# A hybrid decoder block: cross-attention's transposes one step later, three PSUM banks for attention's output product, and the second feed-forward product's first operands in another order

## Chip, cores and metric

The kernel runs on one core of a Trainium2 chip. The metric is device time in microseconds, the median of the runs of one program. A core has TensorE (matmuls, here PE, with its weight loads PEld), VectorE (DVE), ScalarE (ACT), GpSimd (POOL) and SyncE (SP), whose queue issues nearly all DMAs of this kernel. Each engine takes its instructions in the order of its own queue.

## The reference, cut to what matters

One layer on a sequence of 1024 tokens of width 1024, with 256 memory tokens, all in float32:

```python
u = rms_norm(h, norm_mix);  proj = u @ w_in            # parts for both branches and the gates
out_a = GLU of a diagonal state-space branch
att   = forgetting_attention(q, k, v, f_logit)          # 8 heads of 64
out_b = att @ w_fox_o                                   # "attention's output product"
h = h + (gate_a * out_a + gate_b * out_b) @ w_mix_out   # "mix product"
n = rms_norm(h, norm_mem_q); m = rms_norm(mem, norm_mem_kv)
s = (n @ w_q)(m @ w_k)^T * 128**-0.5                    # 4 heads of 128, 256 memory tokens
h = h + (softmax(s) @ (m @ w_v)) @ w_mem_o              # cross-attention
f_a, f_b = split(rms_norm(h, norm_ffn) @ w_ffn_in)      # first feed-forward product
h = h + (silu(f_a) * f_b) @ w_ffn_out                   # second feed-forward product, 2816 x 1024
out = rms_norm(h, norm_final)
```

## The kernel before

Every float32 matrix product is made of three matmuls: each operand is split into a high half, a cast on ScalarE (L178), and a low half, the subtraction source minus high half, mostly on VectorE (L179). L168, L169 and L170 are the three: high by high, high by low, low by high. PSUM has eight banks of 128 x 512, handed out by name: three "mm", two "sc", two "pv" and one "misc". A bank goes to its next user when its last reader is done.

The program is written in an order that a planner then re-arranges. The planner knows estimated costs, and puts on each engine's queue what it takes to be ready, earlier written work first. After that the order on a queue is fixed. `B.behind(ins)` adds one rule for it: the instructions of the block that run on the engine of `ins` come behind `ins` in that queue; DMAs and the other engines are not bound by it.

**Attention's output product** (`fox_part`, L525 to L539) runs in eight parts of 128 output channels, each in two units of 512 tokens. A unit is 12 matmuls into one bank `po`. VectorE multiplies the bank by the gate (L536), which frees the bank, and adds the other branch (L537); the sum is split into `mx`, the operand of the mix product. The two units of a part take the two "pv" banks in turn. Beside it GpSimd applies the other branch's gates (L1131), and ScalarE and VectorE split the weights of the mix product; the first half of them lies in tiles `whi` and `wlo`, four of each, which the output product's weights use as well.

**Cross-attention** (`cross`) works on two halves of 512 tokens. A half has eight steps, two pairs of heads by four blocks of 128 tokens. A step is `mem_scores` (6 matmuls into an "mm" bank; row maximum on VectorE, L687; two exponentials with sums on ScalarE, L690; reciprocal on VectorE, L692; normalising on GpSimd, L694) and `mem_turn` (four transposes into the "misc" bank, L703, split into `pth` and `ptl`). After the four steps of a pair of heads, `mem_values` multiplies by the values. The first half is woven with the query product of the second half, the second half with the memory output product (`mem_out`, sums at L729) of the first. Then the next normalisation (L193 to L220) and the sums and differences for the first feed-forward product follow.

**The feed-forward products** use a recursive scheme with seven half-size products in place of eight. The first one runs over `NF` = 22 blocks of 128 hidden channels, in `start`, `middle` and `end` (matmuls at L875); `middle` ends with a copy of a bank on ScalarE (L896), which `end` needs before it may go on adding into that bank. The hidden values go to DRAM (`gated`: L925, L932), and sums of the second weights as well (`out_sums`: L946, L947).

The second product takes 77 operands in the order of `seq`: `o_get(m)` loads the hidden values (L998) and the weights (L1004) with two DMAs into a tile `or` and splits it; `o_mm` makes 12 matmuls of it (L1015), three into each of four banks. The first seven operands are asked for before its loop starts, four of them ahead of the last block's `end`:

```python
    for m in range(4):
        o_get(m)
    end(NF - 1)
    for m in range(4, AHEAD):       # AHEAD = 7
        o_get(m)
    gated(NP - 1)
    out_sums(NP - 1, 1)
    gfin = B.bcast_gain(s2, g_fin)
```

and the loop asks for operand `m + AHEAD` when it has done operand `m`.

Of the kernel before, what the change touches and what calls it, by code (L numbers as in the profile page):

```python
# [502 lines left out]
def stage_tail(B, big, s2, sh, x, glu, aT, gate_d, kv_d, w_fox_o, w_mix_out, g_mq, w_mem_q, w_mem_o, g_ffn,  # L503
               w_ffn_in, w_ffn_out, g_fin, out):
    nc, V, A, G, T, S, small, ident = B.nc, B.V, B.A, B.G, B.T, B.S, B.small, B.ident
# [19 lines left out]
    def fox_part(j):  # L525
        if j % 2 == 0:
            fox[j // 2] = B.wblock(w_fox_o, 0, 4, j * P, 2 * P)
        fh, fl = fox[j // 2]
        o = (j % 2) * P
        sg = glu.out.pop(j)  # L530
        for h in range(2):
            cs = slice(512 * h, 512 * h + 512)
            po = B.bank("pv")
            B.gemm_t(po, fh[:, :, o:o + P], fl[:, :, o:o + P], aT, h, 4)
            gb = load(gate_d[D + j * P:D + (j + 1) * P, cs], "gb")
            V.tensor_mul(gb, gb, po)  # L536
            V.tensor_add(sg[:, cs], sg[:, cs], gb)  # L537
            mh, ml = mT.rhs(j, h)
            B.split(mh, ml, sg[:, cs])  # L539
# [8 lines left out]
    for j in range(5, 8):  # L548
        fox_part(j)
# [147 lines left out]
    def mem_turn(hf, b, tt):  # L697
        pe = pes.pop((hf, b, tt))
        if tt == 0:
            pts[b] = [(tmp("pth", F32R), tmp("ptl", F32R)) for _ in range(2)]  # L700
        pt = B.bank("misc")
        for i in range(4):
            T.transpose(pt[:, i * P:(i + 1) * P], pe[:, i * P:(i + 1) * P], ident)  # L703
        for i in range(2):
            hi, lo = [p_.rearrange("p (k c) -> p k c", k=2)[:, :, tt * P:(tt + 1) * P] for p_ in pts[b][i]]
            B.split(hi, lo, pt[:, 2 * i * P:2 * (i + 1) * P].rearrange("p (k c) -> p k c", k=2))

    def mem_values(hf, b):
        if b == 0:
            oT[hf] = [[(bslot if hf else slot)(F32R, n) for _ in range(2)] for n in ("oh", "ol")]  # L710
        oh, ol = oT[hf]
        for i in range(2):
            ps = B.bank("pv")
            for kt in range(2):
                cs = slice(kt * 512 + (2 * b + i) * P, kt * 512 + (2 * b + i + 1) * P)
                ks = slice(512 * kt, 512 * kt + 512)
                B.mm3(ps, vh[:, cs], vl[:, cs], pts[b][i][0][:, ks], pts[b][i][1][:, ks], kt == 0, kt == 1)
            B.split(oh[b][:, i * 512:(i + 1) * 512], ol[b][:, i * 512:(i + 1) * 512], ps)
# [12 lines left out]
    def cross(hf):  # L731
        steps = [(b, tt) for b in range(2) for tt in range(4)]
        fs = []
        for i in range(len(steps) + 1):
            if i < len(steps):
                fs.append(lambda s=steps[i]: mem_scores(hf, *s))
            if i > 0:
                fs.append(lambda s=steps[i - 1]: mem_turn(hf, *s))
                if steps[i - 1][1] == 3:
                    fs.append(lambda b=steps[i - 1][0]: mem_values(hf, b))  # L740
        return fs

    for i, s_ in enumerate((kth, ktl, vh, vl)):
# [143 lines left out]
    def middle(j):  # L887
        b1 = ev[j, "b1"]
        b3 = ev[j, "b3"] = B.bank("pv")
        prod(j, 6, b1, False)  # L890
        a1 = ev[j, "a1"] = sh.half("a1")
        A.copy(a1, b1)
        prod(j, 7, b3, True)
        prod(j, 5, b1, False)
        c1 = ev[j, "c1"] = sh.half("c1")
        A.copy(c1, b1)  # L896
        V.scalar_tensor_tensor(out=c1, in0=c1, scalar=-1.0, in1=b3, op0=ALU.mult, op1=ALU.subtract)

    def end(j):
        b1, b3, a0, a1, c1 = [ev.pop((j, s_)) for s_ in ("b1", "b3", "a0", "a1", "c1")]  # L900
# [72 lines left out]
    for j in range(2, NF):  # L973
        if j > AHEAD_IN:
            start(j)
        end(j - 1)
        w_last(j)
        middle(j)
        if j + 1 < NF:
            w_first(j + 1)  # L980
            w_sums(j + 1)
        f = w_fetch(j + 2) if j + 2 < NF else f
        if j % 2:
            out_fetch(j // 2, f.ins)
        else:
            gated(j // 2 - 1)


    LAST, AHEAD = 4, 7
    ORDER = (1, 2, 6, 7, 5, 4, 3)  # L990
    seq = [(n, p) for n in ORDER for p in range(NP)]
    ops, Hf, fin = {}, {}, {}
# [62 lines left out]
                                   op1=ALU.mult)  # L1055
            S.dma_start(out[t * P:(t + 1) * P, cs], Hf[t][:, cs])

    for m in range(4):
        o_get(m)
    end(NF - 1)  # L1060
    for m in range(4, AHEAD):
        o_get(m)
    gated(NP - 1)
    out_sums(NP - 1, 1)
    gfin = B.bcast_gain(s2, g_fin)
# [1 line left out]
    for m, (n, p) in enumerate(seq):  # L1067
        if n == 3 and p >= NP - LAST:
            break
        for i in range(4):  # L1070
            o_mm(m, i)
        if m + AHEAD < len(seq):
            o_get(m + AHEAD)
        if n < 3 and p in (2, 4, 6, 8):
            t = 4 * (n - 1) + p // 2 - 1
            Hf[t] = slot(name="hf")
            S.dma_start(Hf[t], h_d[t])
        if p == NP - 1:
            for i in range(4):
                o_add(n, i)  # L1080
                if n in (2, 5):
                    square(i if n == 2 else 4 + i, n // 3)
                if n == 2:
                    G.tensor_mul(Hf[i][:, :512], Hf[i][:, :512], gfin[:, :512])
                if n == 4:
                    square(4 + i, 0)
                    finish(4 + i)
# [758 lines left out]
```

## Time and profile before

| | |
|---|---|
| median of 3 runs | 1579.52 us (1578.55 to 1581.72) |
| the profiled execution | 1578.99 us |
| its span, first to last instruction | 1577.3 us |
| granted TensorE clock, mean | 0.990 |
| TensorE busy | 1529.5 us, 97% |
| VectorE, ScalarE, GpSimd busy | 1023.0, 657.7, 264.9 us |

In the rows of the profile, times are in us from the start of the span. A row of the timeline gives start, duration, engine, line, operation, the tile written and those read, the shape, a count, and in brackets how long the engine was idle before it and what released it. A row of the chain of waits gives start, duration and work. A row of the busy times by stage begins with a stretch A:B and its length; then come, for PE, PEld, DVE, ACT and POOL, the busy us with the number of instructions in brackets, and at the end the granted TensorE clock, the share of the DMA engines' time and GB/s. A row of the waits names waiter and releaser, the idle time in all, how often, and the longest.

### The profile page before, as it was taken

What the parts mean: (1) busy time and instruction counts of PE and PEld (TensorE: products, weight loads), DVE (VectorE), ACT (ScalarE), POOL (GpSimd) and SP (SyncE); (2) the same over time, 40 slices, a digit from 0 to 9 for tenths busy, and PEclk for the clock granted to TensorE, in tenths of its full rate; (3) what the DMA queues carried; (4) which work ended last, traced back from release to release, by engine and by line L of the source; (5) the groups of instructions that cost most, each with busy time, mean ns of one, the idle gap of its engine ahead of it and who ended that gap; (6) DMA issues with size and microseconds to landing.
All of it is one profiled execution on the core that took longest, in us unless ns stands there. A gap on an engine that the chain in (4) does not pass through costs nothing.

```text
span 1577.3 us, 20371 instructions
## 1 busy us (share of the span) xinstructions
PE 1529.5 (97%) x7313; PEld 1258.4 (80%) x7313; DVE 1023.0 (65%) x1822; ACT 657.7 (42%) x1177; POOL 264.9 (17%) x343
## 2 busy tenths in 40 slices
PE   7799999999999899999999999999999999999997
PEld 6688888898777578878888788888888888788886
DVE  6756545444788677676455688777777775566555
ACT  6422434323566553232335565333333332354342
POOL 3026653200212124110001200100000000001001
PEclk8999999999999999999999999999999999999999
DMA  8753466332123746368411156554445543896642
GB/s 295 151 106 97 130 116 143 97 119 30 25 45 56 206 121 194 114 206 284 144 28 40 62 206 192 169 164 158 159 155 162 161 148 130 279 391 223 192 155 107
DMA packets 196101, 235.09 MB, mean 149 GB/s; under 512 B 35144, under 2 KB 127208, under 8 KB 195488
## 3 DMA queue, kind: packets, MB, share of 16 engines
q1 hardware_dynamic: 188512, 215.97, 46.6%
q10 hardware_dynamic: 7488, 17.83, 3.0%
q8 instruction: 57, 0.93, 0.2%
q14 instruction: 44, 0.36, 0.1%
HBM read 162.98 MB, written 72.71 MB: 149 GB/s over the span
## 4 chain that ended last, share of the span: by engine, by line
PE 80%; DVE 7%; DMA 5%; ACT 3%; POOL 2%; issue 2%; SPq 0%; POOLq 0%; ACTq 0%; DVEq 0%
PE mm L875 14%; PE mm L168 8%; PE mm L169 8%; PE mm L170 8%; PE pv L875 7%; PE mm L1015 4%; PE sc L875 4%; PE sc L168 3%; PE sc L170 3%; PE sc L169 3%; PE sc L1015 3%; PE pv L1015 3%; PE misc L1015 1%; DMA raw<-in_w_in_dram 1%; DMA raw<-in_w_mem_kv_dram 1%
## 5 line engine op out<-in xcount | busy, mean ns | idle before, releaser
L178 ACT CAST whi<-raw 128x1024 fp32r<-128x1024 f32 (+2 forms) x123 | 114.7, 940 | 176.7 <-PE mm L875 52.8
L179 DVE TENSOR_TENSOR wlo<-raw,whi 128x1024 fp32r<-128x1024 f32 (+2 forms) x120 | 127.7, 1069 | 73.2 <-ACT whi L178 71.3
L168 PE MATMUL mm<-uh,whi 128*128 128x512 f32 x344 | 137.5, 400 | 2.5 <-ACT whi L178 2.4
L179 DVE TENSOR_TENSOR ol<-or,oh 128x1024 fp32r<-128x1024 f32 x73 | 92.1, 1266 | 68.5 <-ACT oh L178 67.5
L170 PE MATMUL mm<-uh,wlo 128*128 128x512 f32 x344 | 135.2, 393 | 0.5 <-DVE wlo L179 0.5
L169 PE MATMUL mm<-ul,whi 128*128 128x512 f32 x344 | 135.4, 394 | 0.0
L178 ACT CAST oh<-or 128x1024 fp32r<-128x1024 f32 x73 | 76.9, 1053 | 104.5 <-PE mm L1015 35.2
L907 POOL TENSOR_TENSOR g<-a,c 128x512 f32<-128x512 f32 x22 | 35.8, 1627 | 386.8 <-ACT a L906 299.0
L1665 POOL TENSOR_TENSOR pl<-pf,ph 128x512 fp32r<-128x512 f32 (+1 forms) x32 | 37.8, 1181 | 242.7 <-DVE ph L1664 173.1
L168 PEld LDWEIGHTS mm<-uh,whi 128*128 128x128 f32 x344 | 65.2, 190 | 14.8 <-ACT whi L178 2.8
L170 PEld LDWEIGHTS mm<-uh,wlo 128*128 128x128 f32 x344 | 64.9, 189 | 14.7 <-DVE wlo L179 1.5
L169 PEld LDWEIGHTS mm<-ul,whi 128*128 128x128 f32 x344 | 65.2, 190 | 11.0
L197 POOL TENSOR_TENSOR r<-ms,mhalf 128x1 f32<-128x1 f32 (+1 forms) x30 | 19.4, 647 | 308.1 <-DVE ms L193 280.8
L1662 ACT ACTIVATE pf<-sc 128x512 f32<-128x512 f32 (+1 forms) x96 | 46.3, 489 | 45.0 <-DVE sc L1658 29.4
L875 PE MATMUL pv<-S3h,we 128*128 128x512 f32 x176 | 57.7, 389 | 0.0
L1131 POOL TENSOR_TENSOR sg<-sg,ga 128x512 f32<-128x512 f32 x16 | 30.5, 1928 | 72.7 <-DVE sg L1124 72.7
L1668 DVE TENSOR_TENSOR pl<-pf,ph 128x512 fp32r<-128x512 f32 (+2 forms) x64 | 35.8, 560 | 10.5 <-ACT ph L1667 9.7
L1015 PE MATMUL mm<-oh 128*128 128x512 f32 x106 | 41.2, 389 | 0.0
L1015 PE MATMUL mm<-ol,oh 128*128 128x512 f32 x106 | 41.2, 389 | 0.0
L1015 PE MATMUL mm<-oh,ol 128*128 128x512 f32 x106 | 41.2, 389 | 0.0
L178 ACT CAST we<-rawb 128x512 fp32r<-128x512 f32 x20 | 12.5, 624 | 68.9 <-PE pv L875 33.8
L168 PE MATMUL sc<-uh,whi 128*128 128x512 f32 x104 | 40.8, 393 | 0.0
(583 smaller groups left out, 4585.0 us busy)
## 6 DMA issues: line engine op xcount, KB each, us to landing
or<-c_d SPq DMA_DIRECT2D x77, 256.0 KB
raw<-in_w_in_dram SPq DMA_DIRECT2D x22, 512.0 KB
wo<-in_w_ffn_out_dram SPq DMA_DIRECT2D x22, 512.0 KB
c_d<-g SPq DMA_DIRECT2D x44, 256.0 KB
t_d<-wo SPq DMA_DIRECT2D x44, 256.0 KB
or<-t_d SPq DMA_DIRECT2D x44, 256.0 KB
rawb<-in_w_ffn_in_dram SPq DMA_DIRECT2D x20, 512.0 KB
raw<-in_w_ffn_in_dram SPq DMA_DIRECT2D x20, 512.0 KB
```

The source lines that it names most:

```text
L168: T.matmul(ps, lh, rh, start=first, stop=False)
L169: T.matmul(ps, lh, rl, start=False, stop=False)
L170: T.matmul(ps, ll, rh, start=False, stop=last)
L178: self.A.copy(hi, src)
L179: (self.G if pool_lo else self.V).tensor_sub(lo, src, f32(hi))
L875: T.matmul(ps, l_[:, k, :], r_, start=first and k == 0 and i == 0, stop=k == 3 and i == 2, skip_group_check=True)
L907: G.tensor_mul(g[:, 512:], a1, c1)
L1015: T.matmul(ps, l_[:, gi], r_[:, 512:], start=n < 3 and p == 0 and k == 0 or n == 7 and p == 0 and k == 0, stop=p == NP - 1 and k == 2, ski ...
L1131: self.B.G.tensor_mul(self.out[j][:, cs], self.out[j][:, cs], ga)
L1662: self.exp = A.activation(pf[:, off:], ps[:, off:], AF.Exp)
L1665: G.tensor_sub(pl[:, off:], pf[:, off:], f32(ph[:, off:]))
L1668: V.tensor_sub(pl[:, off:], pf[:, off:], f32(ph[:, off:]))
```

## The change

1. A unit of attention's output product takes its bank from "pv", "pv" and "misc" in turn, in place of "pv" alone.
2. In the written order of cross-attention, the transposes of a step (and the value product after every fourth) come two steps after its scores, in place of one. Eight steps of scores and eight of transposes remain.
3. Of the second feed-forward product's operands, three (0 to 2) are asked for as before. Operands 3 to 7 are asked for ahead of the last `end`, with their casts behind the last `middle`'s copy in ScalarE's queue; operand 8 right after that `end`, also behind the copy. The loop asks from operand 9 on, so nine operands are asked for before it in place of seven.

```diff
@@ fox_part
-            po = B.bank("pv")
+            po = B.bank(("pv", "pv", "misc")[(2 * j + h) % 3])
@@ cross
-        for i in range(len(steps) + 1):
+        for i in range(len(steps) + 2):
             if i < len(steps):
                 fs.append(lambda s=steps[i]: mem_scores(hf, *s))
-            if i > 0:
-                fs.append(lambda s=steps[i - 1]: mem_turn(hf, *s))
-                if steps[i - 1][1] == 3:
-                    fs.append(lambda b=steps[i - 1][0]: mem_values(hf, b))
+            if i > 1:
+                fs.append(lambda s=steps[i - 2]: mem_turn(hf, *s))
+                if steps[i - 2][1] == 3:
+                    fs.append(lambda b=steps[i - 2][0]: mem_values(hf, b))
@@ middle
-        A.copy(c1, b1)
+        copied = A.copy(c1, b1)
         V.scalar_tensor_tensor(out=c1, in0=c1, scalar=-1.0, in1=b3, op0=ALU.mult, op1=ALU.subtract)
+        return copied
@@ the loop over the blocks
-        middle(j)
+        copied = middle(j)
@@ before the second feed-forward product
-    LAST, AHEAD = 4, 7
+    LAST, AHEAD, EARLY = 4, 7, 9
...
-    for m in range(4):
+    for m in range(3):
         o_get(m)
+    with B.behind(copied):
+        for m in range(3, 8):
+            o_get(m)
     end(NF - 1)
-    for m in range(4, AHEAD):
-        o_get(m)
+    with B.behind(copied):
+        o_get(8)
     gated(NP - 1)
...
-        if m + AHEAD < len(seq):
+        if EARLY <= m + AHEAD < len(seq):
             o_get(m + AHEAD)
```

## The prediction

> **What bounds the kernel now.** I read the page's first part, the waits of TensorE from 550 us on (all three edits lie there), the busy time by stage, and then the rows around each wait. The page:
>
> ```profile
> PE 1529.5 (97%) x7313; PEld 1258.4 (80%) x7313; DVE 1023.0 (65%) x1822; ACT 657.7 (42%) x1177; POOL 264.9 (17%) x343
> ```
>
> TensorE is the bound, so the edits can only pay by removing time in which it stands still. The view of waits, from 550 us to the end (waiter and releaser, us in total, times, longest):
>
> ```profile
> PE mm L875 <- ACT c L896: 1.7, 2, 1.0
> PE pv L168 <- DVE gb L536: 1.7, 2, 1.2
> PE misc L703 <- POOL pe L694: 1.3, 4, 0.5
> PE misc L703 <- DVE ptl L179: 1.1, 1, 1.1
> ...
> PE mm L168 <- ACT pe L690: 0.3, 1, 0.3
> ```
>
> Each edit has its row here: the second is the output product's (L536 reads the "pv" bank), the third to fifth are cross-attention's, half of the first is the hand-over from the first feed-forward product to the second. Two rows of TensorE give the true price of a wait:
>
> ```profile
> 1302.06 2.72 PE pv L875 x12
> 703.27 0.50 PE L168 MATMUL pv<-ath,whi 128*128 128x512 f32 x1 [1.24 <-DVE gb L536]
> ```
>
> Twelve 512-column matmuls take 2.72 us, 0.227 us each, while a row shows a matmul as some 0.39 us long. So a wait costs the idle time shown plus 0.16 us, plus 0.11 us because the first matmul after it takes 0.50 instead of 0.39: 0.27 us on top, and I use that throughout. Now part by part.
>
> **The output product's third bank.** Nothing is added or removed; every third unit of 12 matmuls goes to the "misc" bank, which nobody else uses at that time (the next transposes into it come some 70 us later). So a unit waits for the bank of the unit three before it and no longer for that of two before it. Both waits go at their place:
>
> ```profile
> 693.55 0.50 PE L168 MATMUL pv<-ath,whi 128*128 128x512 f32 x1 [0.44 <-DVE gb L536]
> ```
>
> 0.44 + 1.24 + 2 x 0.27 = 2.2 us. But is that work late next? The rows of the chain, then VectorE and ScalarE, then VectorE's busy time in this stretch:
>
> ```profile
> 690.52 3.52 POOL sg L1131 x2
> 694.43 5.25 DMA raw<-in_w_mix_out_dram
> 715.62 0.28 PE mm L169
> 700.79 1.23 DVE L179 TENSOR_TENSOR wbl<-raw,wbh 128x1024 fp32r<-128x1024 f32 x1 [2.21 <-ACT wbh L178]
> 711.17 0.62 ACT L178 CAST mxh<-sg 128x512 fp32r<-128x512 f32 x1 [1.30 <-DVE sg L537]
> 711.70 1.04 ACT L178 CAST whi<-raw 128x1024 fp32r<-128x1024 f32 x1
> 714.12 1.22 DVE L179 TENSOR_TENSOR wlo<-raw,whi 128x1024 fp32r<-128x1024 f32 x1
> 700.80:715.30 14.50, 13.26 (x59) 10.56 (x57) 14.40 (x20) 6.86 (x9) 0.00 (x0) 1.00 0.97 312
> ```
>
> The bank comes late because VectorE stands 2.21 us in front of a weight split whose DMA landed at 699.68, and that DMA was queued on SP behind a gate load that waited for GpSimd. None of it hangs on the banks. From 700.8 on VectorE is busy 14.40 of 14.50 us, and near the end of this row of work it makes the low half of the last weights of the mix product, 714.12 to 715.34. TensorE reads those at 715.62, 0.28 us later. If TensorE ends the output product 2.2 us earlier and VectorE keeps its order, TensorE arrives at the same weights 2.2 us earlier and waits there. So I put this edit at 0: the wait moves from 703 to about 713. Ends: 2.2 us gained if VectorE's order is re-planned so that the split comes earlier; 1.5 us lost (a second wait like that at 703.27, 1.24 + 0.27) if it is re-planned badly. I take 0 because the last row fixes it: VectorE has 0.1 us to spare.
>
> The Trainium skill, "Perfetto Trace Analysis", section "Matmuls", has the rule for this edit: independent groups should rotate through different PSUM banks, so that one group's evacuation overlaps the next group's matmuls. By it the whole 2.2 us would stay and the sum below would be lower by that much; it is the first rival.
>
> **Cross-attention's transposes.** Score group i (6 matmuls of 256 columns, maximum, exponentials, normalising on GpSimd) is followed by its four transposes one group later in the written order, and two groups later after the change. The number of instructions is the same, no DMA moves, and the planner still picks what is ready. The waits:
>
> ```profile
> 840.98 0.66 PE L703 MATMUL misc<-ident,pe 128*128 128x128 f32 x4 [0.54 <-POOL pe L694]
> 869.83 0.38 PE L168 MATMUL mm<-kv,mqh 128*128 128x256 f32 x1 [0.25 <-ACT pe L690]
> 880.98 0.66 PE L703 MATMUL misc<-ident,pe 128*128 128x128 f32 x4 [0.23 <-POOL pe L694]
> 885.57 0.63 PE L703 MATMUL misc<-ident,pe 128*128 128x128 f32 x4 [1.12 <-DVE ptl L179]
> 889.27 0.66 PE L703 MATMUL misc<-ident,pe 128*128 128x128 f32 x4 [0.34 <-POOL pe L694]
> 899.13 0.66 PE L703 MATMUL misc<-ident,pe 128*128 128x128 f32 x4 [0.20 <-POOL pe L694]
> 839.88 3.04 POOL L694 TENSOR_TENSOR pe<-pe,sm 128x512 f32<-128x512 f32 x3 [34.78 <-DVE sm L692]
> ```
>
> Together 2.68 + 6 x 0.27 = 4.3 us, the most that can come. The first stays: GpSimd's three multiplications in a row show that three score groups were out before the first transposes already, so the written order changes nothing there (0.81 us). The second is a score group waiting for a bank, which the change does not touch (0.52 us). The three small ones of the second half (0.20 to 0.34 us idle) are shorter than a score group in between (6 x 0.113 us, half the price of 512 columns), so they go: 0.77 + 3 x 0.27 = 1.6 us. The large one, 1.39 us, came because VectorE ran a normalisation before the split that frees the one "misc" bank; one group later takes about half of it, 0.7 us. Against that stands the end of each half: the last three transposes, not two, now follow with no scores between them, through one bank.
>
> ```profile
> 902.62 0.60 PE L703 MATMUL misc<-ident,pe 128*128 128x128 f32 x4
> 905.19 0.63 PE L703 MATMUL misc<-ident,pe 128*128 128x128 f32 x4
> 907.13 0.42 DVE L179 TENSOR_TENSOR ptl<-misc,pth 128x256 fp32r<-128x256 f32 x1 [0.44 <-ACT pth L178]
> ```
>
> One turn holds the bank from 905.19 to 907.55, 2.4 us. Its cover is the other matmuls that are ready, 24 of the memory output product in the second half, 5.4 us, and as many of the query product in the first; without that cover an extra turn costs the 2.4 us in each half. I charge 0.5 us for a cover that is not perfect. Sum: 1.6 + 0.7 - 0.5 = 1.8 us gained; ends 4.3 gained and the third rival's loss.
>
> **The hand-over.** ScalarE's rows, with those of TensorE, of the queue and of the chain (the row with a stretch counts the matmuls of L1015 in it, 7):
>
> ```profile
> 1349.09 2.81 DMA or<-in_w_ffn_out_dram
> 1352.00 1.05 ACT L178 CAST oh<-or 128x1024 fp32r<-128x1024 f32 x1 [4.19 <-DMA or<-in_w_ffn_out_dram]
> 1352.95 0.58 ACT L896 COPY c<-mm 128x512 f32<-128x512 f32 x1
> 1353.58 0.50 PE L875 MATMUL mm<-S4h,wdh 128*128 128x512 f32 x1 [0.97 <-ACT c L896]
> 1350.80:1353.50 2.70, 1.75 (x7) 1.15 (x7) 1.00 0.70 205
> 1368.91 0.42 SPq L1004 DMA_DIRECT2D or<-in_w_ffn_out_dram  x1
> 1374.77 1.05 ACT L178 CAST oh<-or 128x1024 fp32r<-128x1024 f32 x1 [14.06 <-DMA or<-in_w_ffn_out_dram]
> 1375.85 1.24 DVE ol L179
> 1377.13 0.50 PE L1015 MATMUL sc<-ol,oh 128*128 128x512 f32 x1
> ```
>
> The copy at L896 must be done before the last two products of the first stage can start. It stood in ScalarE's queue behind a cast that waited for a DMA until 1351.90, so TensorE, which had filled in seven matmuls of the second product, still lost 0.97 + 0.27 = 1.24 us. After the change the casts of operands 3 to 8 stand behind the copy: the wait goes, and the fill covers the copy's 0.58 us. What now queues behind the copy: six casts of 1.05 us (6.3 us) and six subtractions of 1.24 us (7.4 us). TensorE first needs operand 3 after two products and 36 matmuls, 60 x 0.227 = 13.6 us later, one more operand each 2.72 us; covered. The SiLU of the last block may wait for one cast, 1.05 us; what it feeds is read a whole product later.
>
> Operands 7 and 8, four DMAs, move on SP's queue from behind the last stores and the load of the final gain to ahead of them. Before, operand 7's weights were issued at 1368.91 and its split ended at 1377.09, so TensorE lost 0.13 us of idle time plus 0.27: 0.4 us, which goes. Operand 9 then is the first behind those stores; issued as before near 1369 and ready by 1377.1, it is needed at about 1380.7 (the products end at 1353.58 + 24 x 0.227 - 1.24 = 1357.8, then come nine operands of 2.72 us less the seven matmuls done ahead): 3.6 us to spare. Sum 1.64 us; I take 1.5. Ends: 1.65 gained, 1.2 lost (the copy's wait again, behind a cast that the planner put wrongly).
>
> **The sum.** 0 + 1.8 + 1.5 = 3.3 us. The profiled execution took 1578.99 us (span 1577.3 and 1.7 around it), so 1575.7; the median of the runs is 0.5 above that execution, so 1576.2. Does a gain at 900 reach the end? Stages after it:
>
> ```profile
> 828.00:909.40 81.40, 78.73 (x414) 64.03 (x415) 48.88 (x125) 43.74 (x131) 18.51 (x20) 1.00 0.16 60
> 926.00:965.00 39.00, 38.74 (x187) 31.91 (x186) 37.17 (x83) 24.19 (x62) 1.48 (x2) 1.00 0.72 245
> 947.00:1346.00 399.00, 398.28 (x1758) 329.39 (x1757) 287.81 (x416) 148.94 (x250) 31.96 (x20) 1.00 0.51 163
> ```
>
> VectorE is full from 926 to 965 (37.17 of 39 us), but with work that TensorE's results start, so it shifts along; after it TensorE runs without holes for 399 us at half the DMA's capacity.
>
> **Rivals.** *First: the third bank keeps its gain.* For it: the rule above, and VectorE's 2.21 us of idle time, which another order would use. Against it: the 0.28 us between split and use. 2.2 us more: 1574.0.
>
> *Second: the cross-attention edit does nothing.* For it: the planner had scores three ahead of the transposes at 840, and picks by what is ready, so the written distance may not bind; the waits are real delays that it did not foresee. Only the hand-over stays, 1.5 us: 1578.0, no measurable change.
>
> *Third, slower: the value product of each half is late.* The last turn of a half moves one place back; the last three stood at 899.13, 902.62 and 905.19, so one place is 2.4 to 3.5 us, in two halves 4.7 to 7. The value product and its split start the normalisations, where VectorE has no slack. At 6.2 us in all, none of the 1.8 gained, less 1.5: 1584.2. It decides once the two delays together pass 4.7 us (1.5 for the hand-over, 3.2 for the bound below). For it: the full VectorE from 926; against it: 24 covering matmuls in each half.
>
> **How the numbers follow.** 0.2% (3.2 us) is about what a measurement of this kernel can tell from no change. Chances: forecast 0.38 (own range 1574.5 to 1578, so some 0.26 of it beyond the bound and 0.12 within), first rival 0.25, second 0.23, third 0.14. Faster 0.26 + 0.25 = 0.51, same 0.12 + 0.23 = 0.35, slower 0.14. The range goes from all three gains in full (2.2 + 4.3 + 1.65 = 8.1 us: 1571.4) to 1581, which leaves out most of the third rival.
>
> **What the next profile would show.** Right: no wait of L168 for L536, and in its place a wait of the mix product for the split at L179 near 713 of about 2 us; fewer and shorter waits at L703 in the second half, the one at 841 still there; ScalarE's copy at L896 directly after the last product that feeds it, casts of operands 3 to 8 behind it, no wait at 1377. Wrong: a mix product that starts 2 us earlier and does not wait; L703 waiting as before, or for L179 at the end of a half; a value product that comes later against the memory output product. Most of all the prediction fails if the planner, fed with a new order, re-sorts the engines' queues at a place that none of the edits names.

## The result, and the profile after

The changed kernel takes 1575.05 us (median of 15 runs), the kernel before, in the same comparison, 1579.38 us. The ratio is 0.9975, 95% interval 0.9965 to 0.9984: 3.9 us faster, between 2.5 and 5.5. Predicted were 1576.2 us and 3.3 us.

The span and the busy time of the engines after, from the page:

```profile
span 1573.4 us, 20367 instructions
PE 1529.7 (97%) x7313; PEld 1260.2 (80%) x7313; DVE 1020.0 (65%) x1822; ACT 658.5 (42%) x1177; POOL 265.7 (17%) x343
```

And the view of TensorE's waits from 550 us to the end, after:

```profile
PE mm L169 <- DVE wlo L179: 1.4, 1, 1.4
...
PE mm L875 <- ACT c L896: 0.7, 1, 0.7
PE misc L168 <- DVE gb L536: 0.6, 1, 0.6
...
PE misc L703 <- POOL pe L694: 0.5, 1, 0.5
...
PE misc L703 <- DVE ptl L179: 0.2, 1, 0.2
```

TensorE does the same work in 3.9 us less span. Each of the three places has changed. The output product's wait for L536 has shrunk from 1.7 to 0.6 us, and a row that was not there before stands above it: the mix product waits 1.4 us for a weight split (L179). The waits at L703 went from 2.4 us in five to 0.7 us in two. The wait for the copy at L896 is there once, not twice; the one left is an early block's, near 975, which no edit touches.

To see which edit paid, I cut both executions at the same landmarks: the first matmul of attention's output product, the last of the mix product, the last group of transposes of cross-attention, the first and the last matmul of the first feed-forward product. The view of busy time by stage, first of before:

```profile
621.78:800.79 179.01, 177.34 (x792) 146.25 (x791) 114.13 (x165) 55.15 (x97) 23.68 (x20) 1.00 0.54 178
800.79:905.55 104.76, 101.99 (x534) 83.39 (x533) 61.15 (x149) 51.11 (x151) 19.06 (x21) 1.00 0.13 45
933.84:1358.93 425.09, 423.14 (x1874) 349.52 (x1873) 308.97 (x451) 163.11 (x277) 35.54 (x23) 1.00 0.53 170
```

The same stretches after:

```profile
622.17:801.37 179.20, 177.15 (x792) 146.29 (x791) 114.54 (x165) 55.14 (x97) 23.88 (x20) 1.00 0.54 178
801.37:903.26 101.89, 101.08 (x534) 84.09 (x533) 60.55 (x149) 51.22 (x151) 20.32 (x21) 1.00 0.13 46
931.51:1354.77 423.26, 422.20 (x1871) 348.96 (x1870) 308.48 (x450) 162.91 (x277) 35.19 (x23) 1.00 0.53 170
```

The second number of each row is what to compare: the third bank's stage is 0.19 us longer, cross-attention's 2.87 us shorter, the hand-over's 1.83 us shorter, 4.5 us in all. The clock was 1.00 in each. The changed execution loses 0.6 us outside these stretches, which leaves the 3.9 us between the spans: 0.39 us before the first landmark, where attention waits once more for ScalarE (0.48 us at 567.15), and 0.24 us behind the last one. This last piece belongs to the hand-over. TensorE's queue has some matmuls of the second feed-forward product ahead of the first one's last, to fill the time of the copy at L896: seven in the kernel before, four in the changed kernel. So 3 x 0.227 = 0.68 us of work only moved behind the landmark, and the hand-over is worth 1.83 - 0.24 = 1.59 us in this pair of executions, not 1.83.

### The profile page after: what moved, and what is told of

The parts are those of the page before. It is cut to its first block, busy times and chain, and to the rows that moved or that the text cites. A ratio compares the mean times of both kernels' runs of the same rounds, so it can differ in the third digit from the quotient of the medians.

```text
span 1573.4 us, 20367 instructions
## 1 busy us (share of the span) xinstructions
PE 1529.7 (97%) x7313; PEld 1260.2 (80%) x7313; DVE 1020.0 (65%) x1822; ACT 658.5 (42%) x1177; POOL 265.7 (17%) x343
## 4 chain that ended last, share of the span: by engine, by line
PE 82%; DVE 6%; DMA 5%; ACT 3%; POOL 2%; issue 2%; SPq 0%; POOLq 0%; ACTq 0%; DVEq 0%
PE mm L875 15%; PE mm L168 8%; PE mm L169 8%; PE mm L170 8%; PE pv L875 7%; PE mm L1016 5%; PE sc L875 4%; PE sc L1016 4%; PE sc L168 3%; PE sc L170 3%; PE sc L169 3%; PE pv L1016 3%; PE misc L1016 2%; DMA raw<-in_w_in_dram 1%; DMA rb<-rd_d 1%
## 5 line engine op out<-in xcount | busy, mean ns | idle before, releaser
L179 DVE TENSOR_TENSOR wlo<-raw,whi 128x1024 fp32r<-128x1024 f32 (+2 forms) x120 | 127.9, 1071 | 71.5 <-ACT whi L178 69.6
L179 DVE TENSOR_TENSOR ol<-or,oh 128x1024 fp32r<-128x1024 f32 x73 | 90.0, 1235 | 73.7 <-ACT oh L178 72.9
L197 POOL TENSOR_TENSOR r<-ms,mhalf 128x1 f32<-128x1 f32 (+1 forms) x30 | 19.5, 650 | 315.2 <-DVE ms L193 282.5
L1016 PE MATMUL mm<-oh 128*128 128x512 f32 x106 | 41.2, 389 | 0.0
L1016 PE MATMUL mm<-ol,oh 128*128 128x512 f32 x106 | 41.2, 389 | 0.0
L1016 PE MATMUL mm<-oh,ol 128*128 128x512 f32 x106 | 41.2, 389 | 0.0
```

The lines of the kernel that those rows point to most:

```text
L179: (self.G if pool_lo else self.V).tensor_sub(lo, src, f32(hi))
L1016: T.matmul(ps, l_[:, gi], r_[:, 512:], start=n < 3 and p == 0 and k == 0 or n == 7 and p == 0 and k == 0, stop=p == NP - 1 and k == 2, ski ...
```

## Experiments

The theory was the prediction's: the third bank's gain is given back at the mix product's weights, cross-attention's edit pays by waits at L703 in the second half, the hand-over's by the wait for the copy at L896 and one for an operand. The rivals: the third bank keeps its gain; the planner, re-sorting, did it all.

One table for all kernels, the lengths of the three stages in us, read from TensorE's rows of each profiled execution in the same way as above:

| kernel | output product to end of mix | to the last transposes | first feed-forward product |
|---|---|---|---|
| before | 179.01 | 104.76 | 425.09 |
| third bank alone | 177.61 | 104.57 | 426.27 |
| cross-attention, second half only | 178.81 | 103.92 | 428.42 |
| cross-attention, first half only | 178.79 | 102.95 | 425.80 |
| cross-attention, both halves | 178.21 | 101.90 | 425.80 |
| roots off GpSimd | 181.00 | 103.74 | 430.04 |
| hand-over alone | 178.17 | 104.66 | 423.26 |
| casts behind the copy only | 177.97 | 104.55 | 423.20 |
| mix interleaved, two banks | 178.03 | 104.61 | 425.57 |
| the change | 179.20 | 101.89 | 423.26 |
| the change, distance three | 179.09 | 104.07 | 423.35 |
| the change, mix interleaved | 176.63 | 102.18 | 423.62 |
| the same, third block's sums held back | 178.31 | 102.10 | 423.22 |
| the same, fourth block's weights held back | 177.68 | 102.00 | 423.34 |

In the first column five kernels that do the same there as the kernel before lie between 177.97 and 178.81, and it at 179.01; the three with the third bank and no interleave spread from 177.61 to 179.20, the three with both from 176.63 to 178.31. So a single execution tells no less than 1.7 us in that stage. The spread is all in TensorE's waits: taking off each wait's idle time and the prediction's 0.27 us, the thirteen executions that ran this stage at clock 1.00 come to 176.6 to 176.8 us. The second column repeats within 0.3 us among kernels with the same cross-attention, the third within 0.5 us where the hand-over is new. Two rows are lengthened by a lower granted clock: that of the roots off GpSimd in its first and third column (0.98 from 700 to 800 us, 0.91 from 1340 to 1380), and the third column of the second half only (0.97 from 1300 to 1360).

**The third bank alone.**

```diff
-            po = B.bank("pv")
+            po = B.bank(("pv", "pv", "misc")[(2 * j + h) % 3])
```

> The third bank alone. Theory: its gain is given back within 15 us, because the mix product then waits for the low half of its last weights on VectorE, which is busy there without a hole. So: TensorE's two waits for L536 shrink (before 0.44 and 1.24 us), a wait of L169 for the split at L179 of 1.4 us or more stands near 716, the last mix matmul is within 0.6 us of its place before, and the time is 0 +- 1 us from before. Rival, the bank is worth what its waits were: 2.2 us faster and no wait near 716.

Measured: 1580.74 us against 1579.64, ratio 1.0003 (0.9991 to 1.0015), as forecast. TensorE's only wait between 640 and 725 us, from its timeline:

```profile
716.35 0.50 PE L169 MATMUL mm<-wlo,mxh 128*128 128x512 f32 x1 [0.78 <-DVE wlo L179]
```

No wait for L536 is left in this execution, and the one that takes its place is for the low half of the mix product's last weights. It is half of the 1.4 us or more that I expected, and the stage (177.61 us) is 0.4 us below the shortest with two banks: by the waits part of the gain was kept here, by the time none shows.

**Two blocks of the mix product interleaved**, in the changed kernel: slices 0 to 5 of the first two token blocks before slices 6 and 7 of both, so that the late weights are needed after 36 matmuls of the product and not after 18, 18 x 0.227 = 4.1 us later. (Not shown below: the product takes a list of slices, and the weaving with the feed-forward weights starts two entries later, which is behind the same token block.)

```diff
+    mixes = [lambda f=f, t=t: f(t) for f in (mix_first, mix_last) for t in range(2)]
-    mixes = [lambda t=t: mix(t, 0, wm0) for t in range(NT)] + ...
+    mixes += [lambda t=t: mix(t, 0, wm0) for t in range(2, NT)] + ...
```

> The changed kernel, with the mix product's first two token blocks interleaved: both take their first six of eight slices of the sum before either takes the last two, which use the weights that are split last. Theory: the 18 more matmuls (4.1 us) cover the wait of 1.42 us (1.7 with its restart) for that split, so the third bank's gain is kept: 1.7 us faster than the changed kernel, 5.5 to 6 faster than before, no wait of L169 near 716. Rival, something else holds the mix product (its other operands, the banks, the DMAs at 97% there): the wait only moves and the time stays at the changed kernel's.

Measured: 1573.67 us, ratio to before 0.9963 (0.9951 to 0.9976), with no wait at all for L536 or for these weights, and the stage at 176.63 us, the shortest seen. By its time it is not told apart from the changed kernel (0.9975, 0.9965 to 0.9984). The two kernels further below that build on it have no wait for these weights either, but one for L536 (0.83 and 1.45 us), and stages of 177.68 and 178.31 us. TensorE's timeline of the one with the third block's sums held back:

```profile
707.98 0.50 PE L168 MATMUL misc<-ath,whi 128*128 128x512 f32 x1 [1.45 <-DVE gb L536]
```

So the interleave takes away the wait for the weights, in three executions of three. Whether the third bank takes away the one for L536 depends on a DMA. Near 700 us VectorE stands in front of a weight split (`wbl`) until a load of the mix product's weights has landed and been cast, and the read at L536 is behind it. These are its idle time there and TensorE's wait for L536 that follows, in us, one pair for each of the fourteen executions:

| | VectorE's idle time: TensorE's wait |
|---|---|
| two banks | 1.24: 0.26, 1.39: 0.42, 1.42: 0.45, 1.53: 0.55, 2.08: 1.10, 2.21: 1.24, 2.74: 1.76, 3.52: 2.55 |
| three banks | 1.35: none, 1.53: none, 2.98: 0.49, 3.14: 0.63, 3.32: 0.83, 3.80: 1.45 |

With two banks TensorE bridges about 1.0 us of this idle time, with three about 2.5. That is what the bank is worth here: 1.5 us of room for a late load, and the earlier wait at 693 (up to 0.45 us), which no execution with three banks has. The idle time was longer in four of the six executions with three banks than in seven of the eight with two; whether the bank makes it so stays open.

**The same interleave with two banks**, as a control.

> The kernel before (two banks for the output product) with the mix product's first two token blocks interleaved, so that the last weights' low half is needed some 2.7 us later. Theory (this pays only together with the third bank, as in the kernel before TensorE loses its time at L536 and not at these weights): from the first output-product matmul to the last mix matmul 178.5 to 179.5 us, as before (179.0); time within 0.5 us. Rival (the interleave is worth its 1.7 us by itself): 177 to 177.6 us, ratio 0.9989.

Measured: 1579.62 us against 1578.96, ratio 1.0007 (0.9996 to 1.0018); two waits for L536, 0.9 us in all, and the stage at 178.03 us, between the theory's 178.5 and the rival's 177.6, among the kernels that change nothing there. (Its expectation put the shift of the need at 2.7 us; it is the 4.1 above.) No run shows either half of the pair paying alone.

**Cross-attention, second half only.**

```diff
+        d = 1 + hf
-        for i in range(len(steps) + 1):
+        for i in range(len(steps) + d):
...
```

> Two steps of distance in the second half of cross-attention alone (first half at one step, no third bank, old hand-over). Theory: nearly all of that edit's gain lies in the second half, where the transposes' waits of 0.20 to 1.12 us were; the last transposes come 2 to 2.5 us earlier than before, and the kernel is 2 to 2.7 us faster. Rival, the first half pays as well or the gain is a re-sorting by chance: less than 1 us here.

Measured: 1578.99 us, ratio 0.9991 (0.9978 to 1.0004). The stage is 0.84 us shorter, a third of what I expected: this expectation fell. The waits that the trace of before shows lie in the second half, and yet changing that half removed little. Three waits stand there in new places (0.62, 0.82 and 0.17 us). The time alone doesn't tell this kernel from the kernel before.

**First half only**, and **both halves**, each in the kernel before.

```diff
-        for i in range(len(steps) + 1):
+        for i in range(len(steps) + (d := 2 - hf)):
...
```

> The kernel before with distance two in the first half of cross-attention only; the second half keeps distance one. Theory 1 (the halves work together): neither half alone gives the gain; the distance from the eighth turn to the last stays within 0.8 us of 36.5, the time within 1 us of before. Theory 2 (the first half's edit alone does it, by what it leaves in the queues for the second): 33.5 to 34.5 us between these turns, time 1576.5 to 1577.5 us. Theory 3 (the two halves add up, 0.7 us from the second): the first half gives about 2 us.

> The kernel before with cross-attention's edit alone, in both halves. Theory 1 (the gain needs both halves together: the first half's edit changes what VectorE and GpSimd have queued when the second half starts): the last turn of transposes stands 2.3 to 2.9 us earlier against the eighth turn than in the kernel before, as in the changed kernel (33.9 us between them, before 36.5), and the time is that much lower, 1576.5 to 1577.3 us (ratio 0.9982 to 0.9987). Theory 2 (part of that gain came from the third bank, which shifted the queues ahead of cross-attention): no more than the second half gave alone, about 0.7 us, ratio 0.9996. The waits of the hand-over and of the output product stay in both.

Measured: first half alone 1577.34 us against 1580.33, ratio 0.9991 (0.9979 to 1.0003), stage 1.81 us shorter. Both: 1575.66 us, ratio 0.9976 (0.9967 to 0.9984), stage 2.86 us shorter, as in the changed kernel (2.87). The time of the first half alone tells no change either; its stage does, since stages with the same cross-attention repeat within 0.3 us. So the edit needs no third bank, and its halves add up within 0.2 us (0.84 + 1.81). Most of the gain comes from the half in which hardly a wait was seen, and it arrives in the other half: up to the eighth of the sixteen groups of transposes, the first-half kernel is only 0.14 us ahead.

The timelines of GpSimd and VectorE in the second half say how. L197 makes a normalisation's reciprocal root on GpSimd, L204 to L206 refine it on VectorE. In the kernel before:

```profile
879.89 1.04 POOL L694 TENSOR_TENSOR pe<-pe,sm 128x512 f32<-128x512 f32 x1 [8.66 <-DVE ms L193]
880.89 0.55 POOL L197 TENSOR_TENSOR r<-ms,mhalf 128x1 f32<-128x1 f32 x1
881.40 1.04 POOL L694 TENSOR_TENSOR pe<-pe,sm 128x512 f32<-128x512 f32 x1
...
881.47 0.99 DVE L204 TENSOR_TENSOR rt<-r 128x1 f32<-128x1 f32 x1 [1.02 <-POOL r L197]
...
882.88 1.28 DVE L220 SCALAR_TENSOR_TENSOR xs<-h,r,gbc 128x1024 f32<-128x1024 f32 x1
884.08 0.41 DVE L179 TENSOR_TENSOR ptl<-misc,pth 128x256 fp32r<-128x256 f32 x1
...
885.01 0.41 DVE L179 TENSOR_TENSOR ptl<-misc,pth 128x256 fp32r<-128x256 f32 x1
```

In the second-half kernel:

```profile
878.55 0.55 POOL L197 TENSOR_TENSOR r<-ms,mhalf 128x1 f32<-128x1 f32 x1
879.07 1.04 POOL L694 TENSOR_TENSOR pe<-pe,sm 128x512 f32<-128x512 f32 x1
...
879.13 0.99 DVE L204 TENSOR_TENSOR rt<-r 128x1 f32<-128x1 f32 x1 [0.81 <-POOL r L197]
```

In the changed kernel:

```profile
878.37 0.55 POOL L197 TENSOR_TENSOR r<-ms,mhalf 128x1 f32<-128x1 f32 x1 [3.24 <-DVE mx L688]
879.90 1.04 POOL L694 TENSOR_TENSOR pe<-pe,sm 128x512 f32<-128x512 f32 x1 [0.98 <-DVE mx L688]
...
879.67 0.14 DVE L204 TENSOR_TENSOR rt<-r 128x1 f32<-128x1 f32 x1
...
880.73 0.23 DVE L205 SCALAR_TENSOR_TENSOR rt<-rt,ms 128x1 f32<-128x1 f32 x1
...
881.32 1.28 DVE L220 SCALAR_TENSOR_TENSOR xs<-h,r,gbc 128x1024 f32<-128x1024 f32 x1
```

Before, the root stands on GpSimd behind the normalising of a score group. VectorE, which keeps its order, stops for 1.02 us, then needs 0.99 us in place of 0.14 for a product of one column, and only after the 1.28 us of L220 comes the split that frees "misc", for which TensorE waits 1.12 us at 885.57. In the changed kernel the planner has put the root ahead of the normalising on GpSimd (L197 at 878.37, L694 at 879.90), and VectorE doesn't stop at L204 (at the next two roots it still does, for 0.58 and 0.66 us). The second-half kernel still has the stop; the first-half kernel, with the root at 878.11 and L204 at 878.74, hasn't. That the first half's order makes the planner queue the second half so is what the runs show; by which of its costs it does stays open.

**The roots off GpSimd**, to try that by itself: the kernel before, distance one, but the roots of the four normalisations beside the second half made by VectorE alone.

```diff
-        B.norm_scale(xs, H[t], B.rstd(H[t]), gf)
+        B.norm_scale(xs, H[t], B.rstd(H[t], t > 3), gf)   # pool=False for t < 4
```

> The kernel before, distance one in both halves; the reciprocal roots of the four normalisations that run beside cross-attention's second half are made by VectorE alone (three refinements from a bit trick, seven small instructions more for each, no instruction of theirs on GpSimd). Theory (what cost the time was VectorE's wait of 1.02 us at L204 for a root that stood on GpSimd behind the normalising of a score group, with the split of the transposes behind it on VectorE; the written distance only moved that): TensorE's wait of 1.12 us at L703 for the split goes, the sum of L703's waits falls from 2.4 to 1.3 us or less, and from the last mix matmul to the last turn 102.9 to 103.7 us instead of 104.8; time 1.1 to 1.9 us below before, ratio 0.9988 to 0.9993. Rival (the distance itself is what counts, as each turn waits for its own chain of maximum, exponentials and normalising): 104.3 us or more, or longer by the 28 added instructions, and the waits for GpSimd at L703 stay four; ratio 0.9997 or above.

Measured: the stage took 103.74 us, 1.02 us less than before, just outside the theory's 102.9 to 103.7 and well short of the rival's 104.3; TensorE's waits at L703 fell from 2.4 to 1.5 us (expected 1.3 or less), those for GpSimd from four to two, and the wait for the split, which the theory took away, from 1.12 to 0.73 us. Taking the roots off GpSimd was worth about 1 us there, against 2.86 for the distance, with 28 more instructions on VectorE in the price. So the stop at the root can account for about that much, and what makes up the rest is not shown. The time, though, was 1580.69 us against 1578.96, ratio 1.0016 (1.0002 to 1.0030), slower, where I expected 1.1 to 1.9 us less. The profiled execution was this kernel's slowest (1589.54 us, granted clock 0.98 from 700 to 800 us and 0.91 at the hand-over), so its other stages can't be held against the kernel before; where the loss lies stays open. (Its wait of 2.80 us for the copy at L896 doesn't settle it, since that wait differs in every kernel with the old hand-over, as told below.) Its timelines of GpSimd and VectorE show one more thing:

```profile
886.24 2.04 POOL L694 TENSOR_TENSOR pe<-pe,sm 128x512 f32<-128x512 f32 x2 [8.64 <-DVE ms L193]
...
886.72 0.58 DVE L204 TENSOR_TENSOR rt<-r 128x1 f32<-128x1 f32 x1
887.33 0.96 DVE L205 SCALAR_TENSOR_TENSOR rt<-rt,ms 128x1 f32<-128x1 f32 x1
888.33 0.16 DVE L206 SCALAR_TENSOR_TENSOR r<-rt,r 128x1 f32<-128x1 f32 x1
```

Two products of one column took 0.58 and 0.96 us, not 0.16, and ended at 887.30 and 888.29, when GpSimd's two multiplications did (886.24 + 1.04 = 887.28, and 888.28). VectorE no longer waits for GpSimd's result but still for GpSimd.

**Distance three** in the changed kernel.

```diff
-            if i > 1:
+            if i > 2:
...
```

> The changed kernel with the transposes three steps behind instead of two. Theory (at two steps the waits are nearly gone: 0.54 and 0.17 us are left at L703, the first not touched by the order): no more than 0.3 us gained, from the last mix matmul to the last turn 101.6 to 102.6 us (101.9 in the changed kernel), time within 1 us of it, ratio to before 0.9970 to 0.9982. Rival (the mechanism of the third rival, value products late): 2 to 3.5 us longer to the last turn of the second half, ratio 0.9985 to 1.000.

Measured: 1576.54 us, ratio to before 0.9988 (0.9978 to 0.9999), the stage 2.2 us longer than at distance two. The rival was right on size, wrong on cause: the last value product of a half follows the half's last transposes at the same distance in both kernels (0.7 us in the first half, 0.8 in the second), so it is late only because they are. At the eighth group of transposes, the end of the first half, this kernel is 2.1 us behind; 1.1 us of that is eight matmuls that only moved ahead of this landmark (352 before it in the changed kernel, 360 here), so some 1.0 us is lost in the first half and 1.2 in the second. The largest waits at L703 in its timeline of TensorE:

```profile
870.88 0.63 PE L703 MATMUL misc<-ident,pe 128*128 128x128 f32 x4 [1.13 <-DVE ptl L179]
...
888.17 0.63 PE L703 MATMUL misc<-ident,pe 128*128 128x128 f32 x4 [0.59 <-DVE ptl L179]
```

Both wait for the split that frees the one "misc" bank, the first where the last groups of the first half follow one another. For this the prediction charged 0.5 us at distance two.

**The hand-over alone**, and **the casts behind the copy only** (operands 3 to 6, still seven ahead).

```diff
# casts only
-    for m in range(4):
+    for m in range(3):
         o_get(m)
+    with B.behind(copied):
+        o_get(3)
     end(NF - 1)
-    for m in range(4, AHEAD):
-        o_get(m)
+    with B.behind(copied):
+        for m in range(4, AHEAD):
+            o_get(m)
```

> The new order of operands alone. Theory: TensorE's waits at 1353.6 (1.24 us with its restart) and 1377.1 (0.40 us) go and nothing takes their place: 1.6 us faster, no wait of TensorE between 1340 and 1380. Rival, the earlier loads and the casts behind the copy make another wait, at operand 9 or at the last products: under 0.8 us faster, with that wait in the trace.

> The kernel before with the casts of operands 3 to 6 put behind the last copy of the first feed-forward product, but still seven operands ahead of the loop. Theory (the hand-over's two waits are separate): TensorE's wait for the copy near 1353 goes, 1.24 us and more; the wait for operand 7 near 1377, 0.13 us idle, stays or grows. Time against before -1.2 us to -4 (as the load in front of the copy was late in the runs compared), from 1340 to 1380 about 0.4 us of excess. Rival (the later issue of the loads undoes it): a wait for operand 4, 5 or 6 of 1 us or more between 1357 and 1377, time as before.

Measured: the hand-over alone 1577.31 us, ratio 0.9989 (0.9979 to 0.9999); the casts only 1577.07 us, ratio 0.9978 (0.9968 to 0.9987). Neither has a wait of TensorE between 1340 and 1380 us. So the wait for operand 7, which I expected to stay with the casts alone, was not tied to the loads' order: it went in that execution too. Whether by the casts or because its DMA landed earlier, these runs don't tell apart; with the old order too it is missing in two executions (third bank alone, and the interleave with two banks). The 40 us of the hand-over in the view by stage, before:

```profile
1340.00:1380.00 40.00, 38.89 (x170) 31.56 (x169) 22.36 (x25) 12.65 (x14) 3.83 (x2) 1.00 0.81 279
```

With the casts only:

```profile
1340.00:1380.00 40.00, 40.00 (x178) 33.00 (x177) 24.22 (x26) 14.60 (x17) 3.83 (x2) 1.00 0.84 304
```

And in the changed kernel:

```profile
1340.00:1380.00 40.00, 40.00 (x178) 33.01 (x177) 24.59 (x26) 13.25 (x15) 3.88 (x2) 1.00 0.84 295
```

178 matmuls in place of 170: 8 x 0.227 = 1.8 us, the 1.64 us of both waits to within a matmul.

**Two tries to take out the early block's wait near 975**, both on top of the interleaved kernel: first the third block's summed weights behind the second block's copy, then the fourth block's weights behind the third's.

```diff
-    middle(1)
-    w_sums(2)
+    with B.behind(middle(1)):
+        w_sums(2)
# the second try, in its place
+        if j == 2:
+            with B.behind(copied):
+                w_first(j + 1)
+                w_sums(j + 1)
```

> The changed kernel with the mix product's first two blocks interleaved (as in the run before of that name) and, as a second edit, the casts of the third block's summed weights in the first feed-forward product put behind the second block's copy on ScalarE. Theory: TensorE's wait for that copy near 974 (0.72 us idle, 0.99 with its restart) goes and nothing takes its place: 1572.7 us, 1.0 below the interleave alone, ratio to before 0.9957. Rival: those weights are read soon after, so that the wait moves to their split; time as with the interleave alone, 1573.7 us, ratio 0.9963.

> The changed kernel with the mix product's first two blocks interleaved, and in the first feed-forward product the casts of the fourth block's weights (not the third's, which did not take the wait away) behind the third block's last copy on ScalarE. Theory: the wait near 974 (0.72 us idle, 0.99 with its restart) goes and none takes its place before 1000; time 1 us below the interleave alone, ratio to before 0.9953 to 0.9960. Rival: the weights held back are late at the fourth block's first products, a wait for them (L834's casts or the subtraction behind) of 0.7 us or more; ratio 0.9960 to 0.9970.

Measured: 1572.56 us, ratio 0.9959 (0.9948 to 0.9971), and 1573.30 us, ratio 0.9967 (0.9954 to 0.9981). In the first the wait stayed (0.73 us at 974.94); in the second it went from there and stood one block later (0.68 us at 986.33). The intervals overlap with each other and with the interleave alone, so both are misses. The interleaved kernels are the fastest of the study, 1.3 to 2.5 us below the change by their ratios (0.9959 to 0.9967 against 0.9975), but all their intervals overlap with that of the change.

## Why the prediction was right, point by point

**Third bank, 0: right in the sum, with luck in it.** A wait moved as forecast, to the low half of the last weights, three microseconds later than the 713 that I named. The timelines of TensorE and VectorE after:

```profile
704.57 0.50 PE L168 MATMUL misc<-ath,whi 128*128 128x512 f32 x1 [0.63 <-DVE gb L536]
...
716.03 0.50 PE L169 MATMUL mm<-wlo,mxh 128*128 128x512 f32 x1 [1.42 <-DVE wlo L179]
...
702.09 1.23 DVE L179 TENSOR_TENSOR wbl<-raw,wbh 128x1024 fp32r<-128x1024 f32 x1 [3.14 <-ACT wbh L178]
...
714.75 1.22 DVE L179 TENSOR_TENSOR wlo<-raw,whi 128x1024 fp32r<-128x1024 f32 x1
...
716.49 1.22 DVE L179 TENSOR_TENSOR wpl<-wpr,wph 128x1024 fp32r<-128x1024 f32 x1
```

The split ends at 714.75 + 1.22 = 715.97 and the matmul starts 0.06 us later, 1.42 us after TensorE was ready. But two steps of the prediction did not hold. It took both waits for L536 away; the one at 704.57, 0.63 us, is what is left of the larger. And it rested the 0 on VectorE keeping its order, which it didn't: the split of `wpl`, for a later stage, stands ahead of the last weights' split in all eight kernels with two banks and behind it in all six with three. VectorE's timeline before:

```profile
711.77 1.23 DVE L179 TENSOR_TENSOR wpl<-wpr,wph 128x1024 fp32r<-128x1024 f32 x1
...
714.12 1.22 DVE L179 TENSOR_TENSOR wlo<-raw,whi 128x1024 fp32r<-128x1024 f32 x1
```

That is the re-planning for which the prediction gave 2.2 us gained. It did not show because VectorE stood 3.14 us for the late load in this execution, before 2.21; so the last split ended 93.80 us after the output product's first matmul, before 93.56. With the bank alone VectorE stood 1.53 us, and it ended at 92.23. The first rival would have kept the 2.2 us; the edit alone gave a ratio of 1.0003, whose interval leaves out the 0.9986 that this would be. The rule of the Trainium skill ("Perfetto Trace Analysis", "Matmuls") on rotating banks is right in its sign here, by the 1.5 us of room in the table above; no run shows it in the time of this kernel by itself.

**Cross-attention, 1.8 us: the sign right, the size short by 1.1 us.** The term failed in three pieces. The wait at 869.83 for a bank, which I left untouched (0.52 us), went. Of the large wait at 885.57 I took half (0.7 of 1.39 us); 0.17 + 0.27 = 0.44 us of it was left, so 0.95 went. And the 0.5 us charged for three turns in a row leaves about 0.2, as a remainder (0.52 + 0.95 + 1.6 for the small waits, less the 2.87 measured). The first wait, at 841, stayed at 0.54 us as I said. Under all three lies one wrong reading: I put the gain where the waits are, in the second half, and the experiments put two thirds of it on the first half's order. That about 1 us of the gain goes through GpSimd's queue is what the kernel with the roots off GpSimd supports. The second rival, that the edit does nothing, fell with the ratio 0.9976 of both halves. The third, late value products, fell too: the last one started at 904.07 us, before at 906.36. (The very first one came 2.7 us later, 53.70 us after the mix product's last matmul and not 51.03, and no wait followed.)

**Hand-over, 1.5 us: right, in mechanism and size.** ScalarE's timeline after:

```profile
1348.78 0.59 ACT L896 COPY c<-mm 128x512 f32<-128x512 f32 x1 [3.97 <-PE mm L875]
1349.26 1.05 ACT L178 CAST whi<-or 128x1024 fp32r<-128x1024 f32 x1
1350.21 3.04 ACT L178 CAST oh<-or 128x1024 fp32r<-128x1024 f32 x3
```

The copy starts as soon as TensorE is done, with the casts behind it. But the wait that it removes depends on when a DMA lands: it was 0.97 us in the profile that I read, and 1.94, 2.70, 1.64, 1.53, 1.42 and 2.80 us in the six other kernels of this study with the old order. The third column of the table goes with it: 423.2 to 423.6 us with the new order, 425.1 to 426.3 with the old where the clock was 1.00. That column overstates the gain, though, because its end is a landmark that the edit itself moves work across. The matmuls of the second product ahead of that end, first those of L1015 before (for PE and PEld only):

```profile
1300.00:1358.93 58.93, 1.75 (x7) 1.31 (x8) 1.00 0.52 176
```

Then those of the same line, L1016, after:

```profile
1300.00:1354.77 54.77, 1.07 (x4) 0.75 (x5) 1.00 0.52 177
```

They are seven in all seven kernels with the old order and four in all seven with the new one. Counted from the first feed-forward product's first matmul to the end of the span, the five executions with the old order and a clock of 1.00 in the first product took 643.4 to 644.2 us, the seven with the new one 641.7 to 642.2: on the mean 1.9 us less, which includes the wait for operand 7. So the edit is worth 1.9 us, near the 1.64 that the prediction added up; the ratio of the hand-over alone, 0.9989, is 1.7 us. Whether it steadies the time as well, spreads of 0.5 us and 0.8 don't tell.

**The sum.** By stages, with the hand-over's 1.59 us, -0.19 + 2.87 + 1.59 = 4.3 us, less the 0.4 lost ahead of them, 3.9 against 3.3 predicted. The forecast came that close because cross-attention's 1.1 us too little is partly cancelled by two losses, the third bank's 0.2 and the 0.4 ahead, that no term named. The edits' own ratios, 1.0003, 0.9976 and 0.9989, give 0.9968 together, inside the interval of the change (0.9965 to 0.9984). The change without its third bank, which by these ratios should take the same time, was not run.

## What to carry to other kernels

Where a bank is added to let one engine run ahead, look for the next thing that it needs: a gain is only kept if that is early too. Here interleaving two units of the next product took that next wait away in three executions of three, and a late load still held up the first one in two of them. A wait is seen on one engine and caused in the queue of another: before pricing a re-ordering, follow the releaser back until you come to an instruction that was ready but stood behind something else. A wait that ends with a DMA has no fixed price: one profile gives one draw of it, here 0.26 to 2.55 us for L536 and 0.97 to 2.80 for L896. And before you price an edit by a stage's length, see whether the edit moves work across the landmark that ends it.

## What the runs showed of the hardware

A product of one column on VectorE, both inputs in SBUF, normally takes 0.14 to 0.16 us. Where GpSimd was in a multiplication at that time it took 0.23, 0.58, 0.96 and 0.99 us, and ended within 0.02 us of GpSimd's end in each case (881.47 + 0.99 = 882.46 and 881.40 + 1.04 = 882.44, above). VectorE's operations with an input in PSUM kept their time: in the changed kernel a split of `ptl` at 879.80 took 0.42 us and a sum at L729 at 880.13 took 0.68, as elsewhere, while GpSimd multiplied from 879.90 to 880.94. The Trainium skill, "SBUF — State Buffer", section "Who interferes with whom", states it: an operation of VectorE with two SBUF inputs contends with a GpSimd operation that reads SBUF, and the later one stops until the first is done. These rows agree, and in the other order too. GpSimd's timeline in the changed kernel:

```profile
881.39 2.10 POOL L694 TENSOR_TENSOR pe<-pe,sm 128x512 f32<-128x512 f32 x1 [0.45 <-DVE r L206]
```

This multiplication started 0.07 us after VectorE's L220 (881.32, 1.28 us, two SBUF inputs) and took 2.10 us instead of 1.04: 1.06 us longer, most of what was left of L220; in the first-half kernel it was 2.11 us, 0.08 us behind an L220. (Where VectorE's operation was a product of 0.16 us, at 886.58 in the changed kernel, a multiplication that started 0.01 us later took 1.05 us: so short a stop doesn't show.) So what stands on GpSimd and VectorE at the same time delays the one that comes second, and that, too, changes when a planner swaps them.
